# DeltaNet's triangular inverse: the first doubling done in compact 32x32 diagonal blocks, turned on VectorE instead of TensorE

## The chip, the cores and the metric

The kernel runs on one core of one Trainium2 chip. The time is device microseconds of one execution; most executions agree within 0.3%. The engines are named as in the profile: PE is TensorE's matrix multiply and PEld its weight load, DVE is VectorE, ACT is ScalarE, POOL is GpSimd, and SP issues the DMAs.

## The reference: one layer of a hybrid decoder

One layer over 1024 prompt tokens (with 16 learned tokens in front) and 8 x 8 tokens of samples in decoding. One input projection (2048 to 8984 columns) feeds six mLSTM heads (A), six gated DeltaNet heads (B) and four HGRN2 heads (C); their outputs are normed, gated and projected back by `w_out`. What matters here is the DeltaNet head, which solves a unit lower triangular system in each chunk of tokens:

```python
A = jnp.where(strict, bc[..., None] * decay * jnp.einsum('nbhtd,nbhsd->nbhts', kc, kc), 0.0)
M = A + jnp.eye(c, dtype=A.dtype)
sol = lax.linalg.triangular_solve(M, rhs, left_side=True, lower=True)
```

## The kernel before

The work is done in two halves of 512 prompt tokens; the first half also carries 80 columns of samples and learned tokens. Hidden states and weights are split into a high and a low part: ACT casts each raw 128x512 piece of weights to `whi`, DVE subtracts to get `wlo`, and PE forms the products `acc<-h,whi` (with the high and the low part of the hidden states) and `acc<-h,wlo`. In the first half a group of six such products belongs to one 128 rows of the contraction, in the second half (`hB`, 512 columns) a group of three. These products make up most of the kernel.

The scans of the heads are generators in queues. After each group `weave.pump()` runs the next step of each queue whose due time has come: a clock kept by the program, with a cost for every instruction (the class `Clock`), sets when a step is due, so that its operands should be there when PE reaches it. What an engine gets is thus one list, in which the small matrix products of a scan stand between groups of `acc`. When a new head starts while two older ones are under way, `weave.drain` runs the older head's remaining steps at once, with no `acc` between them. The scans stand in one queue, so an mLSTM scan starts when the DeltaNet scan ahead of it has been recorded.

A DeltaNet head (`gdn_scan`) inverts M in four chunks of 128 tokens (`main`, NC = 4) and, in the first half, in one tile of 80 (`g.small`). `B` holds the transposed strict part. `substitute()` inverts all 16x16 blocks on the diagonal at once on DVE, in the compact tile `Yc` (128 partitions, 4 or 5 chunks of 16 columns). Then come three doublings, from 16 to 32, 64 and 128. Before the change the first of them works on full 128x128 tiles: `Yc` is expanded into `Y` with a mask, PE turns `Y` into `px` and ACT copies it to `X`, PE multiplies `pz = B.X`, DVE masks it to `Z`, PE multiplies `pyy = Z.Y`, DVE subtracts it from `Y`, and PE and ACT turn `Y` again. The two other doublings (`hh` = 32 and 64) multiply only blocks of that size. In the first half the steps of `first_chain` (`po0`, `pw0`, `po1`, `pu0`, then the update of the sample states, `vx` and `pu`) are taken between them with `next(extra)`. After the inverse, four chunks follow one another with `pr`, `pw`, `pu2` and `po2`.

All helpers record through one line, so nearly every instruction has line 138 (137 after the change); tiles are told apart by their names. A tile that is taken from a shared buffer (`gt`) is named `s` or `t`. In the mLSTM scan, `pst`, `pk`, `pot`, `pum` and `nd` are the PSUM tiles of the scores, of the turned keys, of the turned gate, of the state updates and of numerator and denominator.

Of the kernel before, what the change touches and what calls it, by code (L numbers as in the profile page):

```python
# [6 lines left out]
F32 = mybir.dt.float32  # L7
F32R = mybir.dt.float32r
U8 = mybir.dt.uint8
BF16 = mybir.dt.bfloat16  # L10
AF = mybir.ActivationFunctionType
ALU = mybir.AluOpType
AX = mybir.AxisListType

P = 128
# [176 lines left out]
def hybrid_step(ctx, tc, i, o):  # L192
# [17 lines left out]
    def sq(tag, name, bufs=2, width=P, dtype=F32):  # L210
        return sp.tile([P, width], dtype, tag=tag, name=name, bufs=bufs)
# [6 lines left out]
    def bank(name):  # L218
        return ps.tile([P, 512], F32, tag="ps", name=name)
# [291 lines left out]
    hmask = {}  # L511
    zmask = cp.tile([P, P], BF16, name="zmask")
    m = sq("io", "zm")
    G.memset(m, 0.0)
    v = m.rearrange("p (b x) -> p b x", x=2 * SUB)[:, :, 0:SUB]
    G.memset(v, 1.0)
    G.affine_select(v, v, pattern=[[-2 * SUB, P // (2 * SUB)], [0, SUB]], compare_op=ALU.is_ge, fill=0.0, base=-SUB, channel_multiplier=1)
    G.affine_select(v, v, pattern=[[2 * SUB, P // (2 * SUB)], [0, SUB]], compare_op=ALU.is_ge, fill=0.0, base=2 * SUB - 1, channel_multiplier=-1)
    G.tensor_copy(zmask, m)
    submask = cp.tile([P, P], F32, name="submask")  # L520
    G.memset(submask, 1.0)
    v = submask.rearrange("p (b x) -> p b x", x=SUB)
    G.affine_select(v, v, pattern=[[-SUB, P // SUB], [0, SUB]], compare_op=ALU.is_ge, fill=0.0, base=0, channel_multiplier=1)
    G.affine_select(v, v, pattern=[[SUB, P // SUB], [0, SUB]], compare_op=ALU.is_ge, fill=0.0, base=SUB - 1, channel_multiplier=-1)
    subid = cp.tile([P, SUB], F32, name="subid")
# [619 lines left out]
    def gdn_scan(half, h, ck_, cq, cv, zs, Gb, eG, bb, st):  # L1145
# [74 lines left out]
        yield  # L1220
        Ys, Xs = [], []

        def transpose_Y(g, Y, X):
            n = g.n
            px = bank("px")
            for c in range(g.nt):
                T.transpose(g.psum(px, n)[:, c], Y[0:n, c, 0:n], ident[0:n, 0:n])
            S.copy(X[0:n, :, 0:n], g.psum(px, n))

        def substitute():  # L1230
# [3 lines left out]
            for s_ in range(SUB - 1):  # L1234
# [3 lines left out]
                if s_ in (4, 9):  # L1238
                    ck.last = 0.0
                    yield  # L1240
            for g in gs:
                nb = g.n // SUB
                Y = gt("8", g)
                V.tensor_tensor(Y[0:g.n, :, 0:g.n].rearrange("p c (j t) -> p c j t", t=SUB),
                                Yc[0:g.n, g.idx].unsqueeze(2).to_broadcast([g.n, g.nt, nb, SUB]),
                                submask[0:g.n, 0:g.n].rearrange("p (j t) -> p j t", t=SUB).unsqueeze(1).to_broadcast([g.n, g.nt, nb, SUB]),
                                op=ALU.mult)
                Ys.append(Y)

        vbs, Aqs, kds, rds = [], [], [], []  # L1250
# [65 lines left out]
        yield  # L1316
        Xs = [gt("9", main)]
        transpose_Y(main, Ys[-1], Xs[-1])
        extra = first_chain() if half.first else iter(())
        yield  # L1320
        B, Y, X = Bs[-1], Ys[-1], Xs[-1]
        pz = main.psum(bank("pz"))
        for c in range(NC):
            T.matmul(pz[:, c], B[:, c], X[:, c], start=True, stop=True)
        Z = gt("7", main)
        V.tensor_tensor(Z, pz, zmask.unsqueeze(1).to_broadcast([P, NC, P]), op=ALU.mult)
        next(extra, None)
        yield
        py = main.psum(bank("pyy"))
        for c in range(NC):  # L1330
            T.matmul(py[:, c], Z[:, c], Y[:, c], start=True, stop=True)
        V.tensor_tensor(Y, Y, py, op=ALU.subtract)
        next(extra, None)
        yield
        transpose_Y(main, Y, X)
        next(extra, None)
        yield
        for hh in (32, 64):
            pz = main.psum(bank("pz"))
            Z = gt("7", main)  # L1340
            blocks = [(slice(b, b + hh), slice(b + hh, b + 2 * hh)) for b in range(0, P, 2 * hh)]
            for l, r in blocks:
                for c in range(NC):
                    T.matmul(pz[r, c, 0:hh], B[l, c, r], X[l, c, l], start=True, stop=True)
            for l, r in blocks:
                S.copy(Z[r, :, 0:hh], pz[r, :, 0:hh])
            yield
            py = main.psum(bank("pyy"))
            for l, r in blocks:
                for c in range(NC):  # L1350
                    T.matmul(py[l, c, 0:hh], Z[r, c, 0:hh], Y[r, c, r], start=True, stop=True)
# [475 lines left out]
```

## Time and profile before

| what | value |
|---|---|
| median of 3 runs | 2525.41 us (2525.31 to 2526.97) |
| the profiled execution | 2525.14 us, of which the span is 2523.4 us |
| granted TensorE clock | 0.992 |
| PE busy | 2456.8 us, 97% of the span |
| DVE, ACT, POOL busy | 57%, 40%, 22% |
| DMA | 350.77 MB, 53.9% of 16 engines' span |

The profile gives, for each group of instructions, the busy time, the mean length of one and the idle time of the engine ahead of it with the releaser. A matrix product of plain 32-bit floats appears as two instructions of PE, each with its weight load, so that 4 products count as x8; products of the rounded format (`acc`) and turns with the identity count once. PE's instructions overlap, so what a product costs is read from the starts of the instructions around it.

### The profile page before, as it was taken

The page shows a single profiled execution, that of the slowest core. Times are in us where ns is not written, and L with a number is a line of the kernel's source. Part 1 is how long each engine was busy: PE and PEld are TensorE (multiplying, and loading weights), DVE is VectorE, ACT ScalarE, POOL GpSimd, SP SyncE. Part 2 cuts the span into 40 slices and gives each one's busy share as a digit, 9 for nine tenths or more (in the row PEclk, how much of TensorE's full clock was granted, in tenths as well). Part 3 has the DMA queues.
Part 4 walks back from the last instruction along what each step waited for, and adds up shares of the span by engine and source line. Part 5 has one row for each costly group of instructions (what it writes and reads, how often), then busy time and mean ns, then how long its engine had stood idle before and what let it go on. Part 6 is the DMA issues. An engine that isn't in the chain of part 4 may idle for free.

```text
span 2523.4 us, 43205 instructions
## 1 busy us (share of the span) xinstructions
PE 2456.8 (97%) x15702; PEld 2199.6 (87%) x15702; DVE 1427.0 (57%) x2977; ACT 1012.3 (40%) x2476; POOL 555.0 (22%) x722
## 2 busy tenths in 40 slices
PE   6999999999999999999899999999999999999998
PEld 5899999999999999999687888888888888888886
DVE  7775656765746655556854556554554645323435
ACT  5643434343435333343643434333543334322324
POOL 5331211420314212213320103110320102211201
PEclk9999999999999999999999999999999999999999
DMA  5666655656545454448455445454554548636735
GB/s 129 157 143 147 154 135 122 166 135 133 144 97 143 97 128 115 118 105 225 115 134 122 119 121 130 120 132 100 131 128 111 130 118 264 175 83 195 259 96 184
DMA packets 681041, 350.77 MB, mean 139 GB/s; under 512 B 260004, under 2 KB 622076, under 8 KB 680828
## 3 DMA queue, kind: packets, MB, share of 16 engines
q1 hardware_dynamic: 680828, 348.01, 53.9%
q8 instruction: 123, 2.02, 0.3%
q14 instruction: 90, 0.74, 0.1%
HBM read 285.71 MB, written 62.19 MB: 138 GB/s over the span
## 4 chain that ended last, share of the span: by engine, by line
PE 74%; DMA 6%; issue 6%; DVE 5%; ACT 4%; POOL 3%; SPq 1%; POOLq 0%; DVEq 0%; ACTq 0%
PE acc L138 55%; PE oacc L138 8%; PE pa L138 1%; DVE wlo L138 1%; DMA wraw<-in_w_in_dram 1%; PE po L138 1%; POOL X L138 1%; PE pyy L138 1%; PE pz L138 1%; POOL res L138 1%; ACT whi L138 1%; PE pu L138 1%; ACT L138 1%; PE poh L138 1%; PE nd L138 1%
## 5 line engine op out<-in xcount | busy, mean ns | idle before, releaser
L138 DVE TENSOR_TENSOR wlo<-wraw,whi 128x512 fp32r<-128x512 f32 x720 | 528.4, 738 | 584.9 <-ACT whi L138 566.0
L138 PE MATMUL acc<-hA,whi 128*128 128x288 f32 (+1 forms) x4544 | 823.0, 303 | 11.5 <-ACT whi L138 7.0
L138 ACT CAST whi<-wraw 128x512 fp32r<-128x512 f32 x720 | 441.3, 618 | 879.8 <-PE acc L138 570.2
L138 PE MATMUL acc<-hB,whi 128*128 128x512 f32 x2272 | 723.8, 400 | 4.4 <-ACT whi L138 3.2
L138 PEld LDWEIGHTS acc<-hA,whi 128*128 128x128 f32 x4544 | 678.3, 191 | 17.5 <-ACT whi L138 8.4
L138 PE MATMUL acc<-hA,wlo 128*128 128x288 f32 x2240 | 488.9, 298 | 2.1 <-DVE wlo L138 2.0
L138 PEld LDWEIGHTS acc<-hB,whi 128*128 128x128 f32 x2272 | 411.2, 189 | 84.0 <-ACT whi L138 4.0
L138 PE MATMUL acc<-hB,wlo 128*128 128x512 f32 x1120 | 440.5, 393 | 5.1 <-DVE wlo L138 4.9
L138 PEld LDWEIGHTS acc<-hA,wlo 128*128 128x128 f32 x2240 | 367.1, 190 | 2.9 <-DVE wlo L138 2.9
L138 PE MATMUL oacc<-whi,y 128*128 128x512 f32 x1088 | 344.8, 391 | 1.7 <-ACT whi L138 1.6
L138 PEld LDWEIGHTS acc<-hB,wlo 128*128 128x128 f32 x1120 | 210.6, 188 | 55.9 <-DVE wlo L138 10.4
L138 PEld LDWEIGHTS oacc<-whi,y 128*128 128x128 f32 x1088 | 205.0, 188 | 45.6 <-ACT whi L138 3.4
L138 PE MATMUL oacc<-wlo,y 128*128 128x512 f32 x576 | 225.5, 392 | 2.1 <-DVE wlo L138 2.1
L138 PEld LDWEIGHTS oacc<-wlo,y 128*128 128x128 f32 x576 | 108.6, 189 | 26.1 <-DVE wlo L138 3.9
L138 POOL TENSOR_TENSOR res<-res,fnw 128x512 f32<-128x512 f32 (+1 forms) x34 | 54.3, 1624 | 255.3 <-ACT oscr L138 255.3
L138 POOL TENSOR_TENSOR qd<-qT,emb 128x512 f32<-128x512 f32 x12 | 16.8, 1403 | 355.9 <-PE po L138 355.9
L138 POOL TENSOR_TENSOR y<-y,zs 128x592 fp32r<-128x592 f32 (+1 forms) x32 | 45.5, 1420 | 92.4 <-ACT zs L138 62.8
L138 DVE TENSOR_TENSOR Yt<-Yc,Bb 128x60 f32<-128x60 f32 (+8 forms) x180 | 36.7, 204 | 39.4 <-DMA Bb<-db 34.4
L138 POOL TENSOR_TENSOR hr<-hr,halfneg 128x4 f32<-128x4 f32 (+1 forms) x48 | 47.4, 987 | 46.2 <-DVE hr L138 44.7
L138 POOL TENSOR_TENSOR X<-Ex,hk 128x256 f32<-128x256 f32 (+1 forms) x40 | 38.1, 953 | 87.8 <-PE pa L138 67.9
L138 POOL TENSOR_TENSOR nrm<-nrm,halfneg 128x10 f32<-128x10 f32 x12 | 23.5, 1955 | 122.6 <-DVE nrm L138 122.6
L138 DVE TENSOR_TENSOR Sx<-Sx,lf 128x256 f32<-128x256 f32 (+2 forms) x60 | 36.5, 613 | 20.2 <-ACT Ex L138 19.1
(410 smaller groups left out, 2805.8 us busy)
## 6 DMA issues: line engine op xcount, KB each, us to landing
wraw<-in_w_in_dram SPq DMA_DIRECT2D x564, 256.0 KB
wraw<-in_w_out_dram SPq DMA_DIRECT2D x144, 256.0 KB
y<-y SPq DMA_DIRECT2D x16, 576.0 KB
px<-in_x_prompt_dram SPq DMA_DIRECT2D x32, 256.0 KB
yd<-y SPq DMA_DIRECT2D x128, 64.0 KB
out_dram<-sst SPq DMA_DIRECT2D x16, 512.0 KB
s<-yd SPq DMA_DIRECT2D x32, 256.0 KB
y<-zs SPq DMA_DIRECT2D x32, 256.0 KB
```

The costliest lines, as they stand in the source:

```text
L138: return f(out, *a, **k)
```

## The change

The first doubling no longer uses 128x128 tiles. `Yc` is expanded only to `Y2`, 32 columns for each chunk, in which each row of 32 partitions holds its own 32x32 block of the diagonal. One DVE transpose of 128x128 turns all 16 of these blocks (it turns each 32x32 square in place) into `X2`. PE multiplies 32x32 blocks: 16 products for `pz`, 16 for `pyy`, four for each quarter of partitions. DVE masks `Z2` and subtracts in tiles of 128x128, turns `Y2` again, and expands it to the full `Y`; POOL clears a 64x64 tile `X` for each chunk and copies two blocks into it. The doubling `hh` = 32 reads `X2` and `Y2`, and forms the turned product only for the upper half. The separate step for the first turn is gone, and `next(extra)` is called six times instead of five: once behind each of the first two sets of products, then in the middle and at the end of each later doubling. The masks made at the start change: `zmask` goes, `smallmask`, `evenodd` and `lowleft` come, and DVE sums `even` into `evenodd`.

The diff, without the import that falls away and the rest of `substitute` and the masks:

```diff
...
-    G.affine_select(v, v, pattern=[[SUB, P // SUB], [0, SUB]], compare_op=ALU.is_ge, fill=0.0, base=SUB - 1, channel_multiplier=-1)
+    blocks_of(submask, 2 * SUB, 2 * SUB)
+    smallmask = cp.tile([P, NT0], F32, name="smallmask")
+    blocks_of(smallmask, SUB, SUB)
+
+    evenodd, lowleft = (cp.tile([P, 2 * SUB], F32, name=n) for n in ("evenodd", "lowleft"))
+    even = sq("io", "even")
+    blocks_of(even, SUB, SUB)
+    V.tensor_reduce(evenodd, even.rearrange("p (b y) -> p y b", y=2 * SUB), op=ALU.add, axis=AX.X)
+    G.memset(lowleft, 0.0)
+    G.tensor_copy(lowleft[:, 0:SUB], evenodd[:, SUB:2 * SUB])
...
-        Ys, Xs = [], []
-
-        def transpose_Y(g, Y, X):
-            n = g.n
-            px = bank("px")
-            for c in range(g.nt):
-                T.transpose(g.psum(px, n)[:, c], Y[0:n, c, 0:n], ident[0:n, 0:n])
-            S.copy(X[0:n, :, 0:n], g.psum(px, n))
+        Ys = []
+        Y2, X2 = (sp.tile([P, NC, 2 * SUB], F32, tag=t, name=t, bufs=1) for t in ("Y2", "X2"))
+
+        def turn_Y():
+            V.transpose(X2.rearrange("p c t -> p (c t)"), Y2.rearrange("p c t -> p (c t)"))
+
+        def expand(dst, src, mask):
+
+            n, nt, nb, w = dst.shape
+            V.tensor_tensor(dst, src.unsqueeze(2).to_broadcast([n, nt, nb, w]),
+                            mask.rearrange("p (j t) -> p j t", t=w).unsqueeze(1).to_broadcast([n, nt, nb, w]), op=ALU.mult)
 
         def substitute():
             Yc = sp.tile([P, 5, SUB], F32, tag="Yc", name="Yc", bufs=1)[:, 0:C]
@@ -1238,14 +1246,12 @@
                 if s_ in (4, 9):
                     ck.last = 0.0
                     yield
-            for g in gs:
-                nb = g.n // SUB
-                Y = gt("8", g)
-                V.tensor_tensor(Y[0:g.n, :, 0:g.n].rearrange("p c (j t) -> p c j t", t=SUB),
-                                Yc[0:g.n, g.idx].unsqueeze(2).to_broadcast([g.n, g.nt, nb, SUB]),
-                                submask[0:g.n, 0:g.n].rearrange("p (j t) -> p j t", t=SUB).unsqueeze(1).to_broadcast([g.n, g.nt, nb, SUB]),
-                                op=ALU.mult)
+            expand(Y2.rearrange("p c (e t) -> p c e t", t=SUB), Yc[:, main.idx], evenodd)
+            turn_Y()
+            if half.first:
+                Y = gt("8", gs[0])
                 Ys.append(Y)
+                expand(Y[0:NT0, :, 0:NT0].rearrange("p c (j t) -> p c j t", t=SUB), Yc[0:NT0, 0:1], smallmask[0:NT0])
 
         vbs, Aqs, kds, rds = [], [], [], []
 
@@ -1314,25 +1320,29 @@
         yield from substitute()
         ck.last += 8.0
         yield
-        Xs = [gt("9", main)]
-        transpose_Y(main, Ys[-1], Xs[-1])
         extra = first_chain() if half.first else iter(())
-        yield
-        B, Y, X = Bs[-1], Ys[-1], Xs[-1]
-        pz = main.psum(bank("pz"))
-        for c in range(NC):
-            T.matmul(pz[:, c], B[:, c], X[:, c], start=True, stop=True)
-        Z = gt("7", main)
-        V.tensor_tensor(Z, pz, zmask.unsqueeze(1).to_broadcast([P, NC, P]), op=ALU.mult)
+        B = Bs[-1]
+        near = [slice(b, b + 2 * SUB) for b in range(0, P, 2 * SUB)]
+        pz = bank("pz")[:, 0:2 * SUB * NC].rearrange("p (c t) -> p c t", c=NC)
+        for b in near:
+            for c in range(NC):
+                T.matmul(pz[b, c], B[b, c, b], X2[b, c], start=True, stop=True)
+        Z2 = gt("7", main)[:, :, 0:2 * SUB]
+        V.tensor_tensor(Z2, pz, lowleft.unsqueeze(1).to_broadcast([P, NC, 2 * SUB]), op=ALU.mult)
         next(extra, None)
         yield
-        py = main.psum(bank("pyy"))
-        for c in range(NC):
-            T.matmul(py[:, c], Z[:, c], Y[:, c], start=True, stop=True)
-        V.tensor_tensor(Y, Y, py, op=ALU.subtract)
-        next(extra, None)
-        yield
-        transpose_Y(main, Y, X)
+        py = bank("pyy")[:, 0:2 * SUB * NC].rearrange("p (c t) -> p c t", c=NC)
+        for b in near:
+            for c in range(NC):
+                T.matmul(py[b, c], Z2[b, c], Y2[b, c], start=True, stop=True)
+        V.tensor_tensor(Y2, Y2, py, op=ALU.subtract)
+        turn_Y()
+        Y = gt("8", main)
+        expand(Y.rearrange("p c (j t) -> p c j t", t=2 * SUB), Y2, submask)
+        X = gt("9", main)[0:4 * SUB, :, 0:4 * SUB]
+        G.memset(X, 0.0)
+        for b in near[0:2]:
+            G.tensor_copy(X[b, :, b], X2[b])
         next(extra, None)
         yield
         for hh in (32, 64):
@@ -1341,19 +1351,21 @@
             blocks = [(slice(b, b + hh), slice(b + hh, b + 2 * hh)) for b in range(0, P, 2 * hh)]
             for l, r in blocks:
                 for c in range(NC):
-                    T.matmul(pz[r, c, 0:hh], B[l, c, r], X[l, c, l], start=True, stop=True)
+                    T.matmul(pz[r, c, 0:hh], B[l, c, r], X2[l, c] if hh == 32 else X[:, c], start=True, stop=True)
             for l, r in blocks:
                 S.copy(Z[r, :, 0:hh], pz[r, :, 0:hh])
+            next(extra, None)
             yield
             py = main.psum(bank("pyy"))
             for l, r in blocks:
                 for c in range(NC):
-                    T.matmul(py[l, c, 0:hh], Z[r, c, 0:hh], Y[r, c, r], start=True, stop=True)
-                    if hh == 32:
-                        T.matmul(py[r, c, hh:2 * hh], Y[r, c, r], Z[r, c, 0:hh], start=True, stop=True)
+                    y = Y2[r, c] if hh == 32 else Y[r, c, r]
+                    T.matmul(py[l, c, 0:hh], Z[r, c, 0:hh], y, start=True, stop=True)
+                    if l.stop == 32:
+                        T.matmul(py[r, c, hh:2 * hh], y, Z[r, c, 0:hh], start=True, stop=True)
             for l, r in blocks:
                 V.tensor_scalar(Y[l, :, r], py[l, :, 0:hh], -1.0, None, op0=ALU.mult)
-                if hh == 32:
+                if l.stop == 32:
                     V.tensor_scalar(X[r, :, l], py[r, :, hh:2 * hh], -1.0, None, op0=ALU.mult)
             next(extra, None)
             yield
```

Three places show how the lists of the engines change.

PE in the last DeltaNet head of the second half, from the first product after `substitute` (names as above; `hB` is the second half's hidden states). Before:

```order
L138 MATMUL px<-ident,s_22950 128x128 x4
L138 MATMUL acc<-hB_14887,whi 128x512
L138 MATMUL acc<-hB_14888,whi 128x512
L138 MATMUL acc<-hB_14887,wlo 128x512
L138 MATMUL acc<-hB_14676,whi 128x512
L138 MATMUL acc<-hB_14677,whi 128x512
L138 MATMUL acc<-hB_14676,wlo 128x512
L138 MATMUL pz<-s_23045,Ball 128x128 x4
```

After:

```order
L137 MATMUL pz<-X_23039,Ball 32x32 x16
L137 MATMUL acc<-hB_14983,whi 128x512
L137 MATMUL acc<-hB_14984,whi 128x512
L137 MATMUL acc<-hB_14983,wlo 128x512
L137 MATMUL pyy<-Y_23038,s_23235 32x32 x16
L137 MATMUL acc<-hB_14767,whi 128x512
L137 MATMUL acc<-hB_14768,whi 128x512
L137 MATMUL acc<-hB_14767,wlo 128x512
```

Before, a turn, 6 `acc` and 4 products follow one another, and `pyy` and the second turn come further down in the same way, each 6 `acc` behind the last. Now 16 small products, 3 `acc` and 16 small products follow one another, and 9 `acc` stand between these and the next product, `pz` of the doubling 32.

DVE at the same place, from the last subtraction of `substitute` on (`Y_23038` is `Y2`, `X_23039` is `X2`, `vT<-acc` is the evacuation of a finished group). Before:

```order
L138 TENSOR_TENSOR Yc<-Yc,Yt 128x4
L138 TENSOR_TENSOR s_22950<-Yc,submask 128x512
L138 TENSOR_TENSOR wlo<-wraw,whi 128x512 x2
L138 STREAM_TRANSPOSE vT<-acc 128x512
L138 TENSOR_TENSOR wlo<-wraw,whi 128x512
L138 TENSOR_TENSOR s_23071<-pz,zmask 128x512
L138 TENSOR_TENSOR s_22950<-s_22950,pyy 128x512
L138 TENSOR_TENSOR wlo<-wraw,whi 128x512 x2
L138 TENSOR_SCALAR s_22950<-pyy 32x4x32
L138 TENSOR_SCALAR s_23045<-pyy 32x4x32
```

After:

```order
L137 TENSOR_TENSOR Yc<-Yc,Yt 128x4
L137 TENSOR_TENSOR Y_23038<-Yc,evenodd 128x128
L137 STREAM_TRANSPOSE X_23039<-Y_23038 128x128
L137 TENSOR_TENSOR wlo<-wraw,whi 128x512 x2
L137 TENSOR_TENSOR s_23235<-pz,lowleft 128x4x32
L137 STREAM_TRANSPOSE vT<-acc 128x512
L137 TENSOR_TENSOR Y_23038<-Y_23038,pyy 128x128
L137 TENSOR_TENSOR wlo<-wraw,whi 128x512
L137 STREAM_TRANSPOSE X_23039<-Y_23038 128x128
L137 TENSOR_TENSOR s_23259<-Y_23038,submask 128x512
L137 TENSOR_TENSOR wlo<-wraw,whi 128x512
L137 TENSOR_SCALAR s_23259<-pyy 32x4x32
```

The mask of `pz` stands behind two `wlo` and ahead of `vT`, the second turn behind a `wlo`, and the expansion of 128x512 has moved from ahead of the first product to behind the second.

PE in the first half, at the end of the second mLSTM scan (A1), which follows the second DeltaNet head; the row ahead of it is the step with `pot` and `pum`. Before, from `pot` on:

```order
L138 MATMUL pot<-ident,tho 80x128
L138 MATMUL pum<-meta_725,kwall 128x137
L138 MATMUL pum<-s_5279,kwall 128x129 x4
L138 MATMUL nd<-sst,spread_723 32x129 x8
L138 MATMUL nd<-t_5268,t_5218 32x129 x2
L138 MATMUL nd<-t_5268,t_5218 16x129
L138 MATMUL py<-ident,t_5248 128x80
L138 MATMUL nd<-state_A_741,qd 128x129
L138 MATMUL nd<-s_5279,s_5226 128x129
L138 MATMUL nd<-s_5323,qd 128x129
```

After, from the last of the 12 `acc` that now stand behind `pot` and `pum`:

```order
L137 MATMUL acc<-hA_88,wlo 128x288
L137 MATMUL acc<-hA_88,wlo 128x304
L137 MATMUL nd<-sst,spread_729 32x129 x8
L137 MATMUL nd<-t_5265,t_5219 32x129 x2
L137 MATMUL nd<-t_5265,t_5219 16x129
L137 MATMUL acc<-hA_88,whi 128x288
L137 MATMUL acc<-hA_88,whi 128x304
L137 MATMUL acc<-hA_89,whi 128x288
L137 MATMUL acc<-hA_89,whi 128x304
L137 MATMUL acc<-hA_88,wlo 128x288
L137 MATMUL acc<-hA_88,wlo 128x304
L137 MATMUL nd<-state_A_747,qd 128x129
```

Before, all steps from `pot` to the last `nd` (two more pairs of chunks follow the rows shown) stand in one run without `acc`. After, 12 `acc` stand between `pum` and the first `nd` and 6 more between the sample part of `nd` and the chunks. The scans A3 and A5 change in the same way, while in A2 and A4 the run that began ahead of `pot`, with `pst`, now begins at `pot`.

More of the change, by code (lines that the diff above doesn't have):

```diff
@@ L9 @@
 U8 = mybir.dt.uint8
-BF16 = mybir.dt.bfloat16
 AF = mybir.ActivationFunctionType
@@ L511, in hybrid_step, with blocks_of @@
     hmask = {}
[L512 to L519, printed above, removed]
-    submask = cp.tile([P, P], F32, name="submask")
-    G.memset(submask, 1.0)
-    v = submask.rearrange("p (b x) -> p b x", x=SUB)
-    G.affine_select(v, v, pattern=[[-SUB, P // SUB], [0, SUB]], compare_op=ALU.is_ge, fill=0.0, base=0, channel_multiplier=1)
-    G.affine_select(v, v, pattern=[[SUB, P // SUB], [0, SUB]], compare_op=ALU.is_ge, fill=0.0, base=SUB - 1, channel_multiplier=-1)
+    def blocks_of(out, step, width):
+        G.memset(out, 1.0)
+        v = out.rearrange("p (b x) -> p b x", x=width)
+        n = out.shape[-1] // width
+        G.affine_select(v, v, pattern=[[-step, n], [0, width]], compare_op=ALU.is_ge, fill=0.0, base=0, channel_multiplier=1)
+        G.affine_select(v, v, pattern=[[step, n], [0, width]], compare_op=ALU.is_ge, fill=0.0, base=step - 1, channel_multiplier=-1)
+    submask = cp.tile([P, P], F32, name="submask")
+    blocks_of(submask, 2 * SUB, 2 * SUB)
[7 more added lines that the diff above has]
+    G.tensor_copy(lowleft[:, 0:SUB], evenodd[:, SUB:2 * SUB])
     subid = cp.tile([P, SUB], F32, name="subid")
```

## The prediction

> **What bounds the kernel now.** I read the page first, then the table of waits, then the timeline of one DeltaNet head.
>
> ```profile
> span 2523.4 us, 43205 instructions
> ...
> PE 2456.8 (97%) x15702; PEld 2199.6 (87%) x15702; DVE 1427.0 (57%) x2977; ACT 1012.3 (40%) x2476; POOL 555.0 (22%) x722
> ...
> PE 74%; DMA 6%; issue 6%; DVE 5%; ACT 4%; POOL 3%; SPq 1%; POOLq 0%; DVEq 0%; ACTq 0%
> ...
> L138 ACT CAST whi<-wraw 128x512 fp32r<-128x512 f32 x720 | 441.3, 618 | 879.8 <-PE acc L138 570.2
> ```
>
> PE is busy for 97% of the span and has 74% of the chain that ended last; the span is 1.7 us shorter than the profiled execution (2525.14). The last row says which way the stream of weights is paced: ACT's cast of the next piece waits 570.2 us for PE to be done with an older one, so weights wait for PE. Work taken off PE is then worth its length, unless PE waits in its place. Where PE does wait is in the table of waits:
>
> ```profile
> PE nd L138 <- DVE s L138: 4.8, 4, 1.8
> PE pum L138 <- ACT v L138: 2.0, 2, 1.0
> PE nd L138 <- DVE nsT L138: 1.6, 4, 1.1
> PE px L138 <- DVE s L138: 1.1, 1, 1.1
> ```
>
> The columns are us in total, times, and the longest. Three rows are waits in the mLSTM scans (`nd`, `pum`); one is the first turn of a DeltaNet head, which waited once, 1.1 us, for the end of `substitute`. DVE and ACT are not the bound: what the change takes off them (below) is worth nothing by itself.
>
> **The products, step by step.** The timeline of PE in the last DeltaNet head of the second half shows what each insert costs. Columns: start, length, what, how many instructions.
>
> ```profile
> 2041.02 0.40 PE L138 MATMUL acc<-hB,wlo 128*128 128x512 f32 x1
> 2041.25 1.05 PE L138 MATMUL pyy<-s,s 128*128 128x128 f32 x8
> ...
> 2042.61 0.40 PE L138 MATMUL acc<-hB,wlo 128*128 128x512 f32 x1
> 2042.84 0.62 PE L138 MATMUL acc<-hB,whi 128*128 128x512 f32 x2
> 2043.30 0.39 PE L138 MATMUL acc<-hB,wlo 128*128 128x512 f32 x1
> 2043.53 0.60 PE L138 MATMUL px<-ident,s 128*128 128x128 f32 x4
> ...
> 2044.43 0.39 PE L138 MATMUL acc<-hB,wlo 128*128 128x512 f32 x1
> ...
> 2045.13 0.40 PE L138 MATMUL acc<-hB,wlo 128*128 128x512 f32 x1
> 2045.45 0.59 PE L138 MATMUL pz<-s,Ball 32*32 32x32 f32 x16
> ...
> 2046.54 0.40 PE L138 MATMUL acc<-hB,wlo 128*128 128x512 f32 x1
> ...
> 2047.23 0.40 PE L138 MATMUL acc<-hB,wlo 128*128 128x512 f32 x1
> 2047.56 0.60 PE L138 MATMUL pyy<-s,s 32*32 32x32 f32 x32
> ...
> 2048.66 0.40 PE L138 MATMUL acc<-hB,wlo 128*128 128x512 f32 x1
> ```
>
> From one `wlo` to the next with nothing between is 0.69 us (2042.61 to 2043.30). What an insert adds is the distance of the `wlo` around it less 0.69:
> - four products of 128x128: 2042.61 - 2041.02 - 0.69 = 0.90 us (`pz` has the same form, and I give it the same);
> - four turns: 2044.43 - 2043.30 - 0.69 = 0.44 us;
> - `pz` of the doubling 32, 8 products in two squares of the array: 2046.54 - 2045.13 - 0.69 = 0.72 us;
> - `pyy` of the doubling 32, 16 products in four squares, taken in turn: 2048.66 - 2047.23 - 0.69 = 0.74 us.
>
> Removed from each head: 2 x 0.44 + 2 x 0.90 = 2.68 us. Added: two inserts of 16 products of 32x32, in four squares on the diagonal, eight instructions in one square before the next square begins. No row has this form; the nearest is the 0.72 us of `pz`, which does the same with two squares. What two more squares add hangs on how far squares overlap:
>
> ```profile
> 2045.45:2045.60 0.15, 0.15 (x5) 1.00 0.40 75
> ...
> L138 PE MATMUL pz<-s,Ball 32*32 32x32 f32 x192 | 7.0, 194 | 0.0
> ```
>
> The first row counts PE's weight loads of that `pz` in its first 0.15 us: 5, or 0.030 us each, while only the first square is at work. Eight in one square take 0.24 us. All 16 were started within 0.59 - 0.19 = 0.40 us (span of the insert less the length of its last instruction), where one behind the other they need 16 x 0.030 = 0.48 us. So the second square starts while the first is at work, and a further square costs 0.40 - 0.24 = 0.16 us. The new insert is 0.72 + 2 x 0.16 = 1.04 us, two of them 2.08 us, and a head saves 2.68 - 2.08 = 0.60 us; twelve heads (six in each half) 7.2 us. The ends: if four squares overlap as well as in `pyy`, which started twice as many instructions in the same 0.41 us, an insert is 0.74 us and the saving 12 x 1.20 = 14.4 us; if squares follow one another without overlap, an insert is 0.72 + 32 x 0.030 - 0.40 = 1.28 us and the saving 1.4 us. I take 7.2, since `pz` has the same order of squares.
>
> Here a rule speaks against the change. The Trainium skill, page "TensorEngine Tiling (Array Packing)", section "Gotcha 1: PSUM Pressure", says that different row tiles cannot access the same PSUM bank at the same time. All four squares lie in different rows and write one bank, so by that rule the sum would be the 1.4 us end; the two squares of `pz` above also write one bank from different rows, and they overlapped by 0.08 us, so the trace doesn't follow the rule there; no run here shows four.
>
> The doubling 32 loses 4 of its 16 `pyy` products; they go from the second pair of squares, and the first pair (8 instructions each) still sets the length. I count nothing.
>
> **The rest of the change.** DVE, ACT and POOL, by rows of the groups:
>
> ```profile
> L138 DVE TENSOR_TENSOR s<-pz,zmask 128x512 f32<-128x512 f32 x12 | 8.3, 688 | 6.2 <-PE pz L138 6.2
> L138 DVE TENSOR_SCALAR s<-pyy 32x128 f32<-32x128 f32 x48 | 13.8, 287 | 5.9 <-PE pyy L138 4.4
> L138 DVE TENSOR_TENSOR t<-pvb,cols 80x128 f32<-80x128 f32 x6 | 1.7, 283 | 2.7 <-PE pvb L138 2.7
> L138 DVE STREAM_TRANSPOSE vT<-acc 128x224 f32<-128x224 f32 x6 | 2.2, 373 | 0.0
> L138 ACT COPY s<-px 128x512 f32<-128x512 f32 x24 | 14.1, 586 | 28.9 <-PE px L138 28.7
> L138 POOL COPY state_C<-s 128x128 f32<-128x128 f32 x8 | 2.8, 352 | 22.1 <-DVE wlo L138 19.0 <-PE poh L138 3.1
> ```
>
> DVE loses three operations of 512 columns (0.69 each) and one `TENSOR_SCALAR` (0.29), 2.4 us a head. It gains three operations on 128 columns (0.28 each), two turns (under 0.37) and one of 512 columns (0.69): 2.3 us. ACT loses two copies, 1.2 us. None of this is on PE's path. POOL gains a clear and two copies, about 1 us at 0.35 each; `X` is first read by the doubling 64, 9 + 12 `acc` later (nearly 5 us at 0.23 each), and POOL has nothing queued there but the next `vx`. If that cover went, DVE (which writes `X` too) and PE would wait at most that 1 us.
>
> *The first product.* PE now starts on `X2` instead of a turn of `Y`. It waits for one small expansion and one turn (0.28 + 0.37) where it waited for 0.69: the one wait of 1.1 us stays.
>
> *The mask between the two inserts.* Only 3 `acc` stand there now, in five heads of the second half (5 in the other) and 6 in most of the first half's. From the last start of `pz`: its end comes 0.19 us later, the mask takes 0.28, so `Z2` is there after some 0.5 us. PE needs about 0.1 us to change over (0.32 from `wlo` to `pz` above, against 0.23 to a `whi`), then 0.69 for the `acc`, then about 0.1 again: 0.9 us. Slack 0.4. I count nothing; behind a `wlo` that has just begun (0.69) a head would lose 0.3, and twelve heads 3.6 us.
>
> *The mLSTM scans.* The inverse is one step shorter and the steps are nearer, so the next scan, A, starts earlier in the list. In A1, A3 and A5 of the first half the forced run at the end of the scan is gone. What it cost:
>
> ```profile
> 434.09 0.46 PE L138 MATMUL nd<-state_A,qd 128*128 128x129 f32 x2 [0.19 <-DVE nsT L138]
> ...
> 436.25 0.46 PE L138 MATMUL nd<-s,qd 128*128 128x129 f32 x2 [1.02 <-DVE s L138]
> ...
> 639.15 0.47 PE L138 MATMUL pum<-meta,kwall 80*128 80x137 f32 x2 [1.01 <-ACT v L138]
> ```
>
> These are A1's two waits, 1.21 us, and A2's one. With 18 `acc` (2.3 us, if 288 columns take 288/512 of the 0.23 us above) between `pum` and the last `nd`, DVE's chain of states is done in time: 3 x 1.21 = 3.6 us gained. In A2 and A4 the wait at `pum` goes, but the run from `pot` on is now what it was in A1, so 1.01 is traded for 1.21: 0.4 us lost. A0 stays. Net 3.2 us; the ends are 0 (PE waits elsewhere in the same places) and 6.4 (all `nd` waits in the table).
>
> *The start.* DVE's sum of `even` stands ahead of a `wlo` and waits for POOL:
>
> ```profile
> 57.34 0.19 DVE L138 TENSOR_TENSOR lbt<-params 128x4 f32<-128x4 f32 x1
> ...
> 57.68 0.58 POOL L138 TENSOR_SCALAR_AFFINE_SELECT zm<-zm 128x64 f32<-128x64 f32 x1
> ```
>
> POOL's last selection there ends at 58.26, DVE arrives at 57.53. At worst `wlo` and what is behind it come 0.9 us later; splits run three pieces ahead of PE, so I count nothing.
>
> **Sum.** 7.2 + 3.2 = 10.4 us off the profiled 2525.14 gives 2514.7. The median lies 0.27 above the profiled execution, so 2515.0.
>
> **Rivals.**
> - *The squares do not overlap*: 1.4 + 3.2 saved, 2520.8. For it: four row groups into one bank is more than any row shows. Against it: two overlapped. The page named above stands for it.
> - *The squares overlap as in `pyy`*: 14.4 + 3.2, 2507.8. Against it: `pz` in the same order did not.
> - *The scans give nothing*: the waits of the forced runs reappear at another product: 2518.2. For it: DVE and ACT do the same work there.
> - *The saving is hidden anyway*: PE reaches the weights earlier and waits for them: 2525. Against it: the cast waits for PE for 570 us.
> - *Slower*: PE waits at the second insert for `Z2`, in every head. DVE has two `wlo` queued ahead of the mask; if the second waits for a cast that PE has only just released, the mask comes after cast, `wlo` and mask (0.62 + 0.69 + 0.28 = 1.6 us), 1.2 beyond the slack, in twelve heads 14.4 us: 2529.4. It decides from 10.4 / 12 = 0.87 us a head. Against it:
>
> ```profile
> 2035.21 1.28 DVE L138 TENSOR_TENSOR wlo<-wraw,whi 128x512 fp32r<-128x512 f32 x2
> ```
>
> These are those two `wlo` in the last head; they ended at 2036.49, ahead of where `pz` will stand.
> - *The change doesn't do what it says* is no rival: the products are in the list as described.
>
> **How the numbers follow.** Within 0.2% (5 us) is what a measurement of this kernel can't tell from no change, so from 2520.4 down is faster. Chances: the sum as it stands 0.55 (2515.0, with 2 us to each side from the slack and the start), scans give nothing 0.13, full overlap 0.09, no overlap 0.12, hidden 0.06, slower 0.05. Faster: 0.55 + 0.13 + 0.09 and a third of no overlap, 0.81. Same: 0.08 + 0.06 = 0.14. Slower 0.05. The range leaves out the hidden and the slower case and most of the full overlap: 2509 to 2521.
>
> **What would show it.** In the profile after: no `px` with the identity in the heads, 24 ACT copies of 0.59 us fewer; each new insert 1.04 us by the distance of its `wlo` rows (0.74 or 1.28 would be the rivals); no wait of PE for `s<-pz,lowleft` over 0.3 us; `nd` waits of PE down from 6.4 us to about 5.3 (A0, A2, A4), and none at `pum`. Wrong would make it a row of PE waiting for `Z2`, for POOL's `X`, or for weights.

## The result and the profile after

| kernel | median | ratio to the kernel before, 95% interval |
|---|---|---|
| before (8 runs beside it) | 2526.19 us (2523.14 to 2530.63) | 1 |
| after (8 runs) | 2512.52 us (2509.60 to 2521.60) | 0.9949 (0.9938 to 0.9960) |

The change saves 13.7 us, 0.5%. The time forecast was 2515.0 us; the profiled execution after took 2513.66 us, its span 2512.0 us, 11.4 us less than the span before. One run differs from the next by several us, and its mean granted clock from 0.988 to 0.994; so a term below is read from rows, and a whole from the ratio.

The page of after: span, busy time, and the cast that showed which way the weights are paced.

```profile
span 2512.0 us, 43999 instructions
...
PE 2441.6 (97%) x16086; PEld 2181.8 (87%) x16086; DVE 1428.0 (57%) x3002; ACT 995.7 (40%) x2448; POOL 570.6 (23%) x761
...
L137 ACT CAST whi<-wraw 128x512 fp32r<-128x512 f32 x720 | 441.8, 618 | 915.6 <-PE acc L137 604.5
```

PE is still the bound and the weights still wait for it (604.5 us instead of 570.2). PE is busy 15.2 us less; DVE is where it was (1428.0 instead of 1427.0), and ACT has lost 16.6 us.

The timeline of PE in the last DeltaNet head, the place that the prediction priced (start, length, what, how many):

```profile
2029.77 0.39 PE L137 MATMUL acc<-hB,wlo 128*128 128x512 f32 x1
2030.09 0.89 PE L137 MATMUL pz<-X,Ball 32*32 32x32 f32 x32
...
2031.48 0.39 PE L137 MATMUL acc<-hB,wlo 128*128 128x512 f32 x1
2031.80 0.89 PE L137 MATMUL pyy<-Y,s 32*32 32x32 f32 x32
...
2033.19 0.40 PE L137 MATMUL acc<-hB,wlo 128*128 128x512 f32 x1
```

The same arithmetic as before, distance of the `wlo` less 0.69: 2031.48 - 2029.77 - 0.69 = 1.02 us for `pz`, and 1.02 us for `pyy`.

The table of waits after, PE's rows that answer to the four shown before, and the weights' (us in total, times, the longest):

```profile
PE pt L137 <- DVE x L137: 13.7, 8, 7.1
...
PE pz L137 <- DVE Yc L137: 6.9, 3, 3.6
...
PE acc L137 <- DVE wlo L137: 4.6, 8, 1.2
PE nd L137 <- DVE s L137: 3.5, 4, 1.8
...
PE pz L137 <- DVE X L137: 1.5, 1, 1.5
PE nd L137 <- DVE dn L137: 1.2, 1, 1.2
PE oacc L137 <- DVE wlo L137: 1.0, 4, 0.3
PE oacc L137 <- ACT whi L137: 0.8, 2, 0.6
```

The same rows of before that the prediction did not show:

```profile
PE pt L138 <- DVE x L138: 11.7, 8, 6.6
...
PE acc L138 <- DVE wlo L138: 6.9, 8, 1.4
...
PE oacc L138 <- DVE wlo L138: 2.1, 4, 1.4
PE oacc L138 <- ACT whi L138: 1.6, 3, 1.0
```

The scans' waits (`nd`, `pum`) went from 8.4 to 4.7 us. New are the two rows of `pz`: the first product of a DeltaNet head waited 6.9 us in three heads and 1.5 us in a fourth, where before the first turn waited 1.1 us once. A third group moved, for which the prediction had no term: PE's waits for `wlo` and, in the output projection (`oacc`), for weights went from 10.6 to 6.4 us.

### The profile page after: what moved, and what is told of

It reads as the page before. It is cut to its first block, busy times and chain, and to the rows that moved or that the text cites. A ratio compares the mean times of both kernels' runs of the same rounds, so it can differ in the third digit from the quotient of the medians.

```text
span 2512.0 us, 43999 instructions
## 1 busy us (share of the span) xinstructions
PE 2441.6 (97%) x16086; PEld 2181.8 (87%) x16086; DVE 1428.0 (57%) x3002; ACT 995.7 (40%) x2448; POOL 570.6 (23%) x761
## 4 chain that ended last, share of the span: by engine, by line
PE 77%; issue 6%; DMA 5%; DVE 5%; ACT 3%; SPq 2%; POOL 2%; POOLq 0%; DVEq 0%; ACTq 0%
PE acc L137 58%; PE oacc L137 8%; PE pa L137 1%; DVE wlo L137 1%; PE po L137 1%; PE pyy L137 1%; PE pz L137 1%; POOL res L137 1%; PE nd L137 1%; DMA wraw<-in_w_out_dram 1%; DMA wraw<-in_w_in_dram 1%; DMA px<-in_x_prompt_dram 1%; PE pu L137 1%; ACT whi L137 1%; PE poh L137 1%
## 5 line engine op out<-in xcount | busy, mean ns | idle before, releaser
L137 PE MATMUL acc<-hA,whi 128*128 128x288 f32 (+1 forms) x4544 | 822.3, 303 | 12.4 <-ACT whi L137 7.2
L137 ACT CAST whi<-wraw 128x512 fp32r<-128x512 f32 x720 | 441.8, 618 | 915.6 <-PE acc L137 604.5
L137 DVE TENSOR_TENSOR Sx<-Sx,lf 128x256 f32<-128x256 f32 (+2 forms) x60 | 40.1, 670 | 17.7 <-ACT Ex L137 16.6
```

The lines of the kernel that those rows point to most:

```text
L137: return f(out, *a, **k)
```

## The experiments

All are compared with the kernel before on the same chip; after stands at 0.9949. A difference of two ratios is uncertain by about 0.0017, 4 us.

**Squares in turn.** In both new inserts the loops are exchanged:

```diff
-        for b in near:
-            for c in range(NC):
+        for c in range(NC):
+            for b in near:
                 T.matmul(pz[b, c], B[b, c, b], X2[b, c], start=True, stop=True)
```

> The changed kernel with the two loops around the 16 products of 32x32 exchanged in both new inserts: chunk outside, quarter of partitions inside, so that the four squares are taken in turn. The list of every engine is otherwise the same. My theory: what a further square costs is a start behind the eight instructions of the one before it, so in turn an insert falls from 1.02 us to the 0.74 us of the old pyy, 24 x 0.28 = 6.7 us, 2512.5 to about 2506 (ratio to the kernel before 0.992). Rival, one bank of PSUM written from four rows of squares cannot be used by them at once: the insert stays at 1.02 us or grows to 1.28, 2512 to 2519.

Measured: 2501.72 us, ratio 0.9911 (0.9896 to 0.9925), 0.38% or 9.6 us below after. PE's timeline at the same head:

```profile
2018.99 0.39 PE L137 MATMUL acc<-hB,wlo 128*128 128x512 f32 x1
2019.31 0.45 PE L137 MATMUL pz<-X,Ball 32*32 32x32 f32 x32
...
2020.27 0.39 PE L137 MATMUL acc<-hB,wlo 128*128 128x512 f32 x1
```

The insert costs 2020.27 - 2018.99 - 0.69 = 0.59 us, less than the 0.74 expected: 24 x (1.02 - 0.59) = 10.3 us, which is the saving measured within its uncertainty. The 32 instructions start within 0.45 - 0.19 = 0.26 us, as long as the 8 of one square take at 0.030 us each: one behind the other, they would need 32 x 0.030 = 0.96 us, so four squares work side by side. They lie in four rows of squares and write one bank of PSUM, so the rival falls, and with it the rule weighed in the prediction (the Trainium skill, page "TensorEngine Tiling (Array Packing)", section "Gotcha 1: PSUM Pressure"): the measurement decides against it. The new inserts were slow in after because of the order of their instructions.

**The first product later.** `ck.last += 8.0` becomes 10.5 in the first three heads:

```diff
-        ck.last += 8.0
+        ck.last += 8.0 + (2.5 if half.first and h < 3 else 0.0)
```

> The changed kernel, with the first product of the first three DeltaNet heads of the first half due 2.5 us later (8.0 becomes 10.5 on the program's clock), some 14 groups' worth of acc. My theory: the changed kernel lost 6.9 us of waits at the first pz in these heads, and the granted clock fell to a half behind two of them, in all about 6.8 + 6.6 + 1.6 = 15 us by the places of the acc; both go, the forced run at A1 comes back (1.2 us, with its clock up to 4): about 11 us less, near 2501. Rival, the waits are only the place at which PE idles in any case (the weights or DVE set the pace there): the waits turn up at other products and the time stays at 2512.5 within 2 us.

Measured: 2507.93 us, ratio 0.9934 (0.9922 to 0.9946), 3.8 us below after, less than its uncertainty. Of the two `pz` rows one is left:

```profile
PE pz L137 <- DVE X L137: 1.2, 1, 1.2
```

The waits at the first product went as expected, 7.2 us of them, and about 2 us turned up at other products: `nd` and `pum` wait 5.8 us instead of 4.7, `pkT` 2.1 instead of 1.2. 11 us was too much: that number took the half clock behind two of the waits for a fixed price, which it is not (see the last section).

**Where the waits at the first product come from.** DVE's timeline of after, within the substitution of the second head and of the third:

```profile
368.68 0.75 DVE L137 SCALAR_TENSOR_TENSOR px<-px,bss,pnw 128x512 f32<-128x512 f32 x1 [1.69 <-DMA pnw<-in_norm_w_dram]
...
583.84 0.75 DVE L137 SCALAR_TENSOR_TENSOR px<-px,bss,pnw 128x512 f32<-128x512 f32 x1 [1.62 <-DMA px<-in_x_prompt_dram]
```

`px` is a piece of the second half's hidden states, prepared by a queue of its own (`bg`). With the list moved, these operations came to stand in the middle of the substitution, and DVE, which works its list in order, stood for 1.7 and 1.6 us on their DMAs. From the first operation of the substitution to the expansion DVE now takes 12.4 us in the second head (359.97 to 372.36) and 13.0 us in the third; before the change, with none of these operations there, it took 8.0 and 8.6 us. In the first head it takes 8.6 us, as before (8.5), but begins 3.3 us later, for a reason that stays open. The experiment holds that queue back from the start of `substitute` to the first product:

```diff
+            if name == "bg" and self.hold and not force:
+                continue
...
+        weave.hold = half.first
         yield from substitute()
         ck.last += 8.0
         yield
+        weave.hold = False
```

> The changed kernel, with the program's queue that prepares the second half's hidden states held back while a DeltaNet head of the first half is in its substitution (from its first instruction to the first product); nothing is removed, and the first product keeps its place in the list. My theory: at the second and third head PE waited at the first pz because DVE, in the middle of the substitution, stood for 1.6 to 1.7 us on a DMA of these preparations and did their 0.7 us operations; without them the waits of 1.66 and 3.64 us and the half clock behind them go, 6 to 12 us less: 2500 to 2506, with the 1.6 us at the first head left as it is. Rival, DVE's total work sets the end there, and the preparations come back later as another wait: 2511 within 2 us.

Measured: 2511.11 us, ratio 0.9947 (0.9934 to 0.9959): no gain that can be measured. But the kernel does not do what it was built for: the operations still stand in the substitution, in the second head at the same place of DVE's list as in after, in the third one place later. Why the hold missed them is not shown; draining an older head passes the hold, which may be the reason. DVE's timeline of this kernel:

```profile
366.65 0.75 DVE L137 SCALAR_TENSOR_TENSOR px<-px,bss,pnw 128x512 f32<-128x512 f32 x1 [0.47 <-DMA pnw<-in_norm_w_dram]
...
577.30 0.75 DVE L137 SCALAR_TENSOR_TENSOR px<-px,bss,pnw 128x512 f32<-128x512 f32 x1 [1.07 <-DMA px<-in_x_prompt_dram]
```

PE's waits at the first product did fall, from 8.4 to 6.0 us. That is not the work of the hold, for they were 5.1 us in a kernel that holds nothing back ("ACT's copies put back", below). The second head in that kernel, on DVE and on PE, and then PE with the hold:

```profile
366.26 0.76 DVE L137 SCALAR_TENSOR_TENSOR px<-px,bss,pnw 128x512 f32<-128x512 f32 x1 [0.90 <-DMA pnw<-in_norm_w_dram]
...
370.76 0.87 PE L137 MATMUL pz<-X,Ball 32*32 32x32 f32 x32 [0.87 <-DVE Yc L137]
```

```profile
371.16 0.87 PE L137 MATMUL pz<-X,Ball 32*32 32x32 f32 x32 [0.44 <-DVE Yc L137]
```

DVE waited 1.69 us for this DMA in after, 0.90 with the copies and 0.47 with the hold, at the same place of its list; PE then waited 1.66, 0.87 and 0.44 us. PE's wait follows DVE's one for one, so in the second head the cause is shown. What it would give to move the operations out of the substitution stays open: the 6 to 12 us expected were not tested.

**Only the turns on DVE.** The kernel before, with `V.transpose` on the full 128x512 tile in place of PE and ACT, and without the first turn's own step:

```diff
-            for c in range(g.nt):
-                T.transpose(g.psum(px, n)[:, c], Y[0:n, c, 0:n], ident[0:n, 0:n])
-            S.copy(X[0:n, :, 0:n], g.psum(px, n))
+            V.transpose(X.rearrange("p c t -> p (c t)"), Y.rearrange("p c t -> p (c t)"))
```

> The kernel before with one part of the change: the two turns of Y are made by DVE on the full 128x512 tile (which turns each 32x32 square in place), without PE and ACT, and the first turn has no step of its own; the products stay 128x128, the masks and the subtraction 128x512. My theory: PE loses 24 x 0.44 = 10.6 us of turns, DVE gains 24 x 0.7 us that lie beside other work, and PE waits about 1 us longer once or twice at the first product: 2526 less 9 to 10, near 2516.5; so the turns are more than all of what the inserts gave (7.7 us), and the compact products cost more than the full ones. Rival, the lighter DVE and ACT are what paid: DVE has 17 us more work here than before and ACT 14 us less, so under 4 us of gain, 2522 or more.

Measured: 2517.97 us, ratio 0.9972 (0.9961 to 0.9983), 7 us below before, between the two expectations, nearer to mine. Its table of waits has

```profile
PE acc L138 <- DVE wlo L138: 7.8, 10, 1.2
PE pz L138 <- DVE s L138: 5.3, 4, 1.9
PE nd L138 <- DVE s L138: 5.2, 4, 1.4
```

and DVE's timeline in the third head of the second half shows what stands ahead of one of the four waits at `pz`, where PE stood for 1.22 us:

```profile
1622.86 0.69 DVE L138 TENSOR_TENSOR s<-Yc,submask 128x512 f32<-128x512 f32 x1
1623.47 0.69 DVE L138 TENSOR_TENSOR wlo<-wraw,whi 128x512 fp32r<-128x512 f32 x1
1624.07 0.70 DVE L138 STREAM_TRANSPOSE s<-s 128x512 f32<-128x512 f32 x1
```

PE loses its 10.6 us of turns, but waits 5.3 us at the first product in four heads: the expansion and the turn take 0.7 us each on the wide tile, and a `wlo` falls between them. In after the same two take 0.29 and 0.31 us, but the first product waits longer there (8.4 us), and the compact products cost PE more than the full ones (1.02 against 0.90 us) as long as the squares are not taken in turn. So neither explains why after is about 6 us (2 to 10) faster than this kernel. What differs in its favour is the list behind: PE's waits in the scans and for weights are 19.1 us in this kernel, as they were before (19.0), and 11.1 us in after.

**ACT's copies put back.**

```diff
             V.transpose(X2.rearrange("p c t -> p (c t)"), Y2.rearrange("p c t -> p (c t)"))
+            nc.scalar.copy(back.rearrange("p c (j t) -> p c j t", t=2 * SUB), X2.unsqueeze(2).to_broadcast([P, NC, 4, 2 * SUB]))
```

> The changed kernel with 24 copies of 128x512 put back on ACT, each behind a turn on DVE and waiting for it as the old copies waited for PE; the copies go to a tile that nobody reads, and they are not counted on the program's clock, so that the list is otherwise the same. My theory: ACT is off the path and what was taken off it is worth nothing: 2511 within 2 us. Rival, part of the 13.7 us came from ACT, whose casts of weights no longer stand behind a copy that waits: 24 x 0.59 us would be up to 14 us, and at least 4 us more should be seen, 2515 or over.

Measured: 2509.06 us, ratio 0.9942 (0.9928 to 0.9955): not slower than after. The 24 copies took 0.62 us each; ACT is not the bound, and what was taken off it gave nothing that can be measured.

**The old list behind the inverse.** Empty steps between the inverse and the four chunks, so that the chunks and the mLSTM scans fall about where they fell before; first in both halves:

```diff
         for _ in extra:
             yield
+        for _ in range(8 if half.first else 4):
+            yield
         vb, Aq, kd = vbs[-1], Aqs[-1], kds[-1]
```

> The changed kernel with eight empty steps (first half) or four (second half) between the inverse and the four chunks, so that the chunks and the mLSTM scans fall at the places in the list that they had before the change; the inverse itself is untouched. My theory: the shorter list of steps gave 3.7 us of nd and pum waits, which come back, with the half clock behind A0's wait (2 us more); the inserts stay: 2512.5 + 4 to 6 = 2517 to 2519. Rival 1, the scans give nothing: no change, 2512.5. Rival 2, most of the gain is the new list of steps and not the cheaper inserts: over 2521.

Measured: 2523.55 us (12 runs, 2516.42 to 2531.49), ratio 0.9996 (0.9985 to 1.0008). The whole gain is gone, 11.9 us (8 to 16), though PE's inserts are those of after. Both my number and the first rival are wrong; the second rival holds as far as the list gave more than was thought. It does not say that the cheaper inserts gave nothing: PE still waits 5.3 us at the first product in this kernel (1.1 before), and the squares in turn show that what an insert saves is saved in the time. Two more kernels have the steps in one half alone:

> The changed kernel with the eight empty steps behind the inverse in the first half alone (the mLSTM scans A0 to A5 fall where they fell before the change; the second half is as after). My theory now: the list behind the inverse gave some 10 us, of which about half are waits of the forced runs of the first half's mLSTM scans: 2511 + 4 to 7 = 2515 to 2518, ratio 0.9965 to 0.998. Rival 1, the first half gave all of it: ratio 0.9995. Rival 2, the first half gave nothing and the second half all: 0.995.

Measured: 2515.98 us, ratio 0.9969 (0.9960 to 0.9979), 5.0 us above after. The waits of the mLSTM scans in it:

```profile
PE nd L137 <- DVE s L137: 4.2, 3, 1.4
...
PE pum L137 <- DVE kwall L137: 2.0, 1, 2.0
...
PE pum L137 <- ACT v L137: 1.0, 1, 1.0
```

They are 7.2 us, where after has 4.7.

> The changed kernel with the four empty steps behind the inverse in the second half alone (its chunks fall where they fell before the change; the first half is as after). My theory now: two waits for wlo (0.9 and 0.8 us) in the second half and one of 1.4 us at the start of the output projection, which the kernel before had and the kernel with both sets of empty steps has again, come back, each with some 0.4 us of lost overlap: 4 to 5 us, ratio 0.9965 to 0.997, and the waits stand at the same three places. Rival, those waits hang on something else (when the second half begins): they do not come back, ratio 0.995.

Measured: 2518.24 us, ratio 0.9985 (0.9972 to 0.9997), 9 us above after (5 to 13), more than expected. The waits came back at the places named:

```profile
1529.07 0.50 PE L137 MATMUL acc<-hB,wlo 128*128 128x512 f32 x1 [0.84 <-DVE wlo L137]
...
1816.40 0.51 PE L137 MATMUL acc<-hB,wlo 128*128 128x512 f32 x1 [0.92 <-DVE wlo L137]
...
2121.89 0.50 PE L137 MATMUL oacc<-wlo,y 128*128 128x512 f32 x1 [1.41 <-DVE wlo L137]
```

Before the change the first of them stood so on PE:

```profile
1533.46 0.39 PE L138 MATMUL acc<-hB,wlo 128*128 128x512 f32 x1
...
1535.20 0.50 PE L138 MATMUL acc<-hB,wlo 128*128 128x512 f32 x1 [0.89 <-DVE wlo L138]
```

and so on DVE, where that `wlo` began only at 1533.92, behind a scan of the HGRN2 heads that waits for ACT (`Sx<-Sx,lf`):

```profile
1532.70 0.42 DVE L138 TENSOR_TENSOR Sx<-Sx,lf 128x256 f32<-128x256 f32 x1 [1.08 <-ACT Ex L138]
...
1533.92 1.22 DVE L138 TENSOR_TENSOR wlo<-wraw,whi 128x512 fp32r<-128x512 f32 x1
```

From `wlo` to `wlo` are 1.74 us, 1.05 more than the 0.69 without a wait: a wait of 0.89 costs 1.05, since the overlap with the product ahead is lost as well. Three such waits explain about 4 of the 9 us. The rest is not placed; the granted clock may have a part, for its mean was 0.985 to 0.988 in the four of the 11 runs that took over 2521 us, and 0.989 to 0.994 in the others (2512.0 to 2519.0).

**All small products in turn.** The same exchange also in the doublings 32 and 64:

```diff
-            for l, r in blocks:
-                for c in range(NC):
+            for c in range(NC):
+                for l, r in blocks:
                     T.matmul(pz[r, c, 0:hh], B[l, c, r], X2[l, c] if hh == 32 else X[:, c], start=True, stop=True)
```

> The kernel with the two new inserts taken square by square in turn, and the same exchange of loops in the doublings 32 and 64: pz of the doubling 32 in two squares in turn, its pyy in three squares in turn. My theory, from the insert of 0.59 us that 16 products in four squares in turn now took: what sets the length is the instructions in one square (eight) at 0.030 us each, so pz and pyy of the doubling 32 fall from 0.72 and 0.73 to about 0.6 each, 12 x 0.26 = 3.1 us: ratio 0.990. Rival, 0.59 was special to four squares (PE hides the loads of three others), and two in turn gain nothing: ratio 0.991.

Measured: 2495.10 us, ratio 0.9884 (0.9871 to 0.9898). `pz` of the doubling 32, with the `wlo` around it:

```profile
2013.37 0.40 PE L137 MATMUL acc<-hB,wlo 128*128 128x512 f32 x1
2013.70 0.44 PE L137 MATMUL pz<-X,Ball 32*32 32x32 f32 x16
...
2014.64 0.40 PE L137 MATMUL acc<-hB,wlo 128*128 128x512 f32 x1
```

It costs 0.58 us instead of 0.72, and `pyy` 0.58 instead of 0.73; two squares in turn gain as well. The rows are worth 12 x 0.29 = 3.5 us. The ratio fell by 6.8 us from that of the squares in turn, uncertain by 5 us, which allows for the 3.5.

**Both together.** All products in turn, and the queue held back.

> Both together: all small products in turn, and the preparation of the second half held back during the substitutions. My theory: the two add up where the wait at the first product is left: in the kernel with the inserts in turn that wait was 5.1 us with one half clock behind it, so 4 to 7 us below that kernel and about 3 below for the doubling 32: ratio 0.988 to 0.989. Rival, they do not add, because the list behind shifts and forced runs of mLSTM scans come back: ratio 0.991.

Measured: 2493.34 us, ratio 0.9878 (0.9864 to 0.9891), 1.2% below before, 0.7% below after. Against the products in turn alone it gains nothing that can be measured. Nor could it show whether the two add up: here too `px<-px` stands in the substitution of the second and of the third head, behind waits of 0.67 and 0.97 us for DMAs.

## Why the prediction was right, and where only by chance

| term, us | predicted | read from the rows before and after |
|---|---|---|
| products and turns, 12 heads | -7.2 | -7.7 |
| waits of the mLSTM scans | -3.2 | -3.7, and about -2.0 of lost overlap |
| wait at the first product | 0 | +7.3 |
| waits for weights (`wlo`, `oacc`) | 0 | -4.2, and about -0.7 of lost overlap (four waits by 0.16) |
| start (`pt`) | 0 | +2.0 |
| sum | -10.4 | -9.0 of the 11.4 that the span lost |

*The products.* The mechanism and the size were right: 1.02 us where 1.04 was worked out, 12 x (2.68 - 2.04) = 7.7 us. The reason given, that a further square costs the time from the end of one group of starts to the next, was confirmed when the order was changed; the end that the prediction took from `pyy` (0.74) was not an end, since in turn the insert came to 0.59. The kernel before was itself written in the slow order at the doubling 32.

*The scans.* In part this is luck. In A1, A3 and A5 the mechanism was right: the run without `acc` is gone, with its 3.6 us of waits, and nothing waits at `pum` any more. But A0, which was to stay, waits once for 1.2 us where it waited twice for 2.9, and A2 and A4, which were to lose 0.4 us, lost 1.5, of which 1.0 in A2. A0's wait after, then the longer of A2's:

```profile
292.92 0.49 PE L137 MATMUL nd<-s,qd 128*128 128x129 f32 x2 [1.16 <-DVE dn L137]
...
647.97 0.49 PE L137 MATMUL nd<-s,qd 128*128 128x129 f32 x2 [1.76 <-DVE s L137]
```

The two misses nearly cancel, so that 3.7 us of idle time came near the 3.2. PE's timeline has A1's chunks after,

```profile
435.88 0.38 PE L137 MATMUL nd<-state_A,qd 128*128 128x129 f32 x2
...
437.58 0.76 PE L137 MATMUL acc<-hA,whi 128*128 128x288 f32 x4
```

and the end of the same run before, which began at 434.09:

```profile
437.48 0.48 PE L138 MATMUL pu<-vx,k 128*128 128x512 f32 x1
```

The eight `nd` steps, four chunks of two, take 437.58 - 435.88 = 1.70 us now; before they took 437.48 - 434.09 = 3.39. The 1.69 between them is more than the 1.02 that the table of waits gave for the longer wait in this stretch, and with the 0.19 ahead of it 0.7 us more than the term of 1.21 for one scan, 2.0 us for three: mis-sized, because a wait was priced by its idle time alone.

*The first product: the step that failed.* The prediction said "the one wait of 1.1 us stays", and compared only the two operations at the end of the substitution. It did not ask what the moved steps put into DVE's list before that end: the operations on `px` made the substitution of the second and third head over 4 us longer. In the profiled execution the waits cost 7.3 us; with the same products on PE they cost 4.0 us in the kernel with ACT's copies put back, so the size changes from execution to execution. The one experiment that took most of these waits away gained 4 us, less than its uncertainty, so no more than a few us of this is shown in the time.

*What went unmentioned.* PE's waits for weights fell by 4.2 us, as a by-product of the moved list: the empty steps put three of them back at the same places. Together with the scans, the list behind the inverse is worth 11.9 us (8 to 16), more than the term of 3.2. A gain and a loss that were both left out stood against each other, and that is why the sum came within 3 us of the median.

*What was counted at nothing and was nothing.* No wait of PE for `Z2` or for POOL's `X` is in the table; ACT's lost copies gave nothing (put back, the time stayed). DVE's sum into `evenodd` ran at 57.18 us and waited for nothing that the profile shows. The 2.0 us that `pt` waited longer are not its doing, for those waits end at 42.6 us; in the kernel with all products in turn, which has the same start, `pt` waited 12.1 us, 0.4 more than before.

About 2.4 us of the span are not placed, and the granted clock does not explain them. It was 0.73 behind the wait of the scan A0 before (292 to 296 us) and 1.00 there after, but behind the first product of the third head after it was 0.62 (588 to 592 us), and the mean was 0.992 before and 0.991 after.

## What to carry to other kernels

Small products in different squares of the array should be issued in turn, square after square, not one square's set behind another's: the same 16 products cost 0.59 us instead of 1.02 here, in one bank. In a kernel whose list is set by due times, a shorter step moves everything behind it, and what that does (here 11.9 us, 8 to 16) can exceed what the step itself saves (7.7 us): read the moved list of every engine, not only at the step but up to the next wait on both sides. Before a shorter wait is put down to a change, see whether the list at that place changed at all: here the same list gave waits of 8.4 us in one kernel and 5.1 us in another. A wait costs its idle time plus the lost overlap, which was 0.16 us behind one of 0.89 here and 0.7 us for two waits of 1.21 in a run of small products.

## What the runs showed of the hardware that was not expected

The granted clock fell to a half behind some waits of PE and not behind others, with no length that separates them. After the wait of 1.66 us in the second head of after, the clock was 0.50, and a row of four `acc` took 1.33 us where it took 0.71 ahead of the wait; the wait of 1.62 us in the first head left it at 1.00 (232 to 236 us), and so did the wait of 3.54 us in the kernel with all products in turn. PE's timeline of after, then the window (the granted clock is the third number from the end):

```profile
373.17 0.87 PE L137 MATMUL pz<-X,Ball 32*32 32x32 f32 x32 [1.66 <-DVE Yc L137]
...
374.33 1.33 PE L137 MATMUL acc<-hA,whi 128*128 128x288 f32 x4
```

```profile
374.00:378.00 4.00, 4.00 (x45) 3.65 (x44) 1.12 (x4) 0.00 (x0) 0.00 (x0) 0.50 0.60 119
```

PE's timeline, then the window, of the kernel with all products in turn:

```profile
579.47 0.45 PE L137 MATMUL pz<-X,Ball 32*32 32x32 f32 x32 [3.54 <-DVE Yc L137]
```

```profile
580.00:584.00 4.00, 4.00 (x60) 3.79 (x59) 2.79 (x9) 1.82 (x6) 0.27 (x1) 1.00 0.60 121
```

The Trainium skill, page "TensorE: Matmul & The Clock Gate", section "What's actually happening", has the clock halved after at least one idle window of about 3.4 us; here it was halved behind an idle time of 1.66 us. What decides is not shown, so no price for a wait can be taken from one such loss, as I did for the first product in the experiments.
